# Recurrent-state products on all 128 rows of the matrix engine, and expert results added there: one change to a two-layer hybrid network kernel

## The chip, the cores and the metric

The kernel runs on one core of a Trainium2 chip, as one program of 39,137 instructions. The core has a matrix engine (PE, whose weight loads are listed apart as PEld), three engines for elementwise work (DVE, ACT and POOL), and a sync engine (SP) that here only issues DMAs. The metric is the device time of one execution in microseconds; smaller is better.

## The reference

Two layers over 512 latent and 256 context tokens of width 1024. The parts that the change touches:

```
def gla_scan(q, k, v, la, state):          # 4 heads, keys of 32, values of 64, chunks of 64 tokens
    def step(S, xs):
        b = jnp.cumsum(lc, axis=-2)
        inter = jnp.einsum('bhld,bhde->bhle', qc * jnp.exp(b), S)
        ...
        h = inter + jnp.einsum('bhls,bhse->bhle', att, vc)
        S = jnp.exp(b[..., -1, :])[..., None] * S + jnp.einsum('bhsd,bhse->bhde', kc * jnp.exp(b[..., -1:, :] - b), vc)

def mlstm_scan(q, k, v, ig, lf, state):    # 4 heads of 64
        num = a[..., None] * jnp.einsum('bhld,bhde->bhle', qc, C) + jnp.einsum('bhls,bhse->bhle', s, vc)

def hybrid_layer(...):
    ...
    y = hier_moe(...)                      # every token: the sum of two experts' weighted results
    x_l = post_norm(DN_ALPHA * x_l + g2_l * y_l.reshape(B, S, D), p['ln_ffn_g'], p['ln_ffn_b'])
```

Both scans run over the tokens in both directions (context first, then latents), and the two directions' results are added. Layer 0 gives outputs for all 6 tiles of 128 tokens, layer 1 for the 4 latent tiles only.

## The kernel before

**Order.** The program is written as generators ("threads") that a small planner (`Sched`, `Thread`, `run`) steps by estimated ready times. Beside the gated linear attention (`gla`, called GLA here) and the mLSTM run the input projections (`projections`: long rows of `mm<-whi,hT` matmuls) and the conditioning (`ada`: `mm<-wa,cs`). A compile-time scheduler then fixes the order of each engine's instructions by a simulated timeline. On the chip each engine goes through its own list in order.

**GLA.** `gla_span` does 256 tokens in one direction: four chunks of 64. Head pairs lie on partition halves: rows 0 to 63 hold heads 0 and 1 (g = 0), rows 64 to 127 heads 2 and 3 (g = 1). DVE forms the decays, PE the per-chunk products `pu`, and DVE the chain of states `glS` (lines 1130 to 1139). Then, for each tile of 128 tokens, chunk `cc` and half `g`, two matmuls add into one PSUM region (lines 1179 to 1183): the masked scores `A` (tile `gA`) by the values `v2`, over 128 rows, and the decayed queries `qs` (`Fqs`) by the state that entered the chunk, over the 64 rows of the half:

```
r = slice(64 * g, 64 * g + 64)
nc.tensor.matmul(o, A[:, 2 * g + cc]..., self.v2[:, t, cc, g, :], start=True, stop=ent is None)
nc.tensor.matmul(o, qs[r, 2 * u + cc]..., ent[r, :], start=False, stop=True)
```

**mLSTM.** `mlstm` first runs the states `C` (`mC`) over six tiles in both directions, then goes tile by tile: for each direction and head a 128-row matmul `PT x va` (`mE` by `mva`) and a 64-row one, `qa x C` (`mqa` by `mC`), into one region (lines 1299 to 1302).

All of these operands are float32. Each float32 matmul of the program is two MATMULs, each with a weight load of its own, in the trace.

**End of a layer.** `final_phase` loads, for each tile of 128 tokens, the results of the two experts (`y0`, `y1`; between the layers they lie in spare buffers named `whi`, `wlo`, `wr`), adds them on POOL (line 2151), multiplies by the gate `g2` in layer 0, and does the residual, the norm and (in layer 0) the modulated norm for the next layer. There are 6 tiles after layer 0 and 4 after layer 1. The pool `big` has two PSUM buffers of 128 x 1024.

`tt` and `cp` choose an engine by the planner's clocks (`pick`).

Of the kernel before, what the change touches and what calls it, by code (L numbers as in the profile page):

```python
# [51 lines left out]
def host_consts():  # L52
    import numpy as np
    cols, off, state = [], {}, {"n": 0, "g": None}

    def add(name, a):
        a = np.asarray(a, np.float32)
        if a.ndim == 1:
            a = np.broadcast_to(a, (128, a.shape[0]))
        off[name] = (state["g"], state["n"] - off[state["g"]][0], a.shape[1])  # L60
        cols.append(a)
        state["n"] += a.shape[1]
        off[state["g"]] = (off[state["g"]][0], state["n"] - off[state["g"]][0])

    def group(g):
        state["g"] = g
        off[g] = (state["n"], 0)

    p = np.arange(128)
    group("base")  # L70
    add("ident", np.eye(128))
    add("mk", (p // 32 % 2)[:, None] == np.arange(2)[None, :])
    group("gla")
    add("r64", np.tile((np.arange(64) > 0), 4))
    add("r8", np.tile((np.arange(8) > 0), 32))
    s, l = (p % 64)[:, None, None], np.arange(64)[None, None, :]
    same = (p // 64)[:, None, None] == np.arange(2)[None, :, None]
    for d in range(2):
        a, b = (s, l) if d == 0 else (l, s)
        ms = [(s // 8 == l // 8) & (a <= b)]  # L80
        for w in (8, 16, 32):
            ms.append((s // (2 * w) == l // (2 * w)) & (a // w % 2 == 0) & (b // w % 2 == 1))
        group(f"gm{d}")
        for n, m in enumerate(ms):
            add(f"gm{d}{n}", (m & same).reshape(128, 128))
    group("ml")
    add("negf", np.where(p[:, None] <= p[None, :], 0.0, NEG))
    add("negb", np.where(p[:, None] >= p[None, :], 0.0, NEG))
    for q in range(2):
        sel = np.zeros((128, 128))  # L90
        for m in range(128):
            for d in range(2):
                sel[DB * d + 2 * q + m // 64, m] = 1
        add(f"sel{q}", sel)
    group("da")
    inv = (np.float32(10000.0) ** (-np.arange(16, dtype=np.float32) / np.float32(16))).astype(np.float32)
    t = np.arange(NL)
    ar = (t // 64).astype(np.float32)[:, None] * inv
    ac = (t % 64).astype(np.float32)[:, None] * inv
    ang = np.concatenate([ar, ar, ac, ac], -1).astype(np.float32)  # L100
    sgn = np.concatenate([-np.ones(16), np.ones(16)] * 2).astype(np.float32)
    add("cos", np.cos(ang).reshape(TL, 128, 64).transpose(1, 0, 2).reshape(128, -1))
    add("sin", (np.sin(ang) * sgn).reshape(TL, 128, 64).transpose(1, 0, 2).reshape(128, -1))
    group("tr2")
    add("tri", p[:, None] < p[None, :])
    add("ones", np.ones((128, 128)))
    group("rt")
    add("io32", np.arange(32))
    add("io4", np.arange(4))
    add("tokb", FAR - (np.arange(TT)[None, :] * 128 + p[:, None]))  # L110
    add("iojb", np.arange(256) - FAR)
    add("pcol", p[:, None])
    e = np.arange(32)
    add("kb", np.where(e < 2, 65536.0, 0.0) + 31 - e)
    add("kbc", (np.where(p < 2, 65536.0, 0.0) + 31 - p)[:, None])
    group("moe")
    add("far2", (2.0 * FAR + p // 64)[:, None])
    add("far4", (4.0 * FAR + p // 32)[:, None])
    add("ioj2", np.arange(128) % 64 - FAR)
    add("ioj4", np.arange(128) % 32 - FAR)  # L120
    add("sum4", (p // 64 * 32 + p % 32)[:, None] == np.arange(64)[None, :])
    add("ce", np.tile(e, NB))
    for i in range(2):
        add(f"cb{i}", (np.array(caps(i))[None, :] + 128 * np.arange(NB)[:, None]).reshape(-1))
    arr = np.ascontiguousarray(np.concatenate(cols, 1).astype(np.float32))
    return arr, off
# [120 lines left out]
class Net:  # L247
# [796 lines left out]
    def gla_span(self, d, t0, carry):  # L1044
# [81 lines left out]
        for x in range(n64):  # L1126
            for g in range(2):
                nc.tensor.matmul(pu[64 * g:64 * g + 64, x * 64:x * 64 + 64], kt[:, x, 64 * g:64 * g + 64],
                                 self.v2[:, tiles[x // 2], x % 2, g, :], start=True, stop=True)
        S = self.fw.tile([128, n64, 64], F32, name="glS")  # L1130
        entry = {}
        for x in (range(n64) if d == 0 else range(n64 - 1, -1, -1)):
            entry[x] = carry
            u = pu[:, x * 64:x * 64 + 64]
            if carry is None:
                V.tensor_copy(S[:, x, :], u)
            else:
                V.scalar_tensor_tensor(S[:, x, :], carry, dec[:, x:x + 1], u, op0=OP.mult, op1=OP.add)
            carry = S[:, x, :]
        self.carry = carry  # L1140
        for u, t in enumerate(tiles if live else []):
            yield (kf, qf)
            G = self.big.tile([128, 2, 512], F32, name="big")
# [10 lines left out]
            for n, w in enumerate((64, 8, 16, 32)):  # L1154
# [14 lines left out]
                for hh in range(2):  # L1169
                    r = slice(64 * hh, 64 * hh + 64)  # L1170
                    V.copy_predicated(Aj[r, :, hh], mj[r, None, hh].to_broadcast([64, 4, y, w]), Gj[r])
            yield (A, S)
            po = self.big.tile([128, 2, 512], F32, name="big")
            for cc in range(2):
                ent = entry[2 * u + cc]
                for g in range(2):
                    o = po[:, g, cc * 64:cc * 64 + 64]
                    r = slice(64 * g, 64 * g + 64)
                    nc.tensor.matmul(o, A[:, 2 * g + cc].rearrange("p a l -> p (a l)"), self.v2[:, t, cc, g, :],
                                     start=True, stop=ent is None)  # L1180
                    if ent is not None:
                        nc.tensor.matmul(o, qs[r, 2 * u + cc].rearrange("p a l -> p (a l)"), ent[r, :],
                                         start=False, stop=True)
            src = po[:, :, 0:128].rearrange("p g (c e) -> p c g e", c=2)
            if d == 0:
                self.cp(self.gl[:, t], src, 256)
            else:
                hh = self.fp.tile([128, 256], F32, name="ghh")
                V.tensor_tensor(hh.rearrange("p (c g e) -> p c g e", c=2, g=2), self.gl[:, t], src, op=OP.add)
                f = lambda x: x.rearrange("p c g e -> p (c g e)")  # L1190
                self.head_out(self.fp, hh, 4, 64, f(rs[t]), f(self.gl[:, t]))
                self.dump(f"gl{self.i}_{t}", f(self.gl[:, t]))

    def head_out(self, pw, hh, nh, w, mul, out):

# [13 lines left out]
    def mlstm(self, pg):  # L1209
# [11 lines left out]
            V.tensor_copy(mdec[d], pd[:, :16].rearrange("p (q n) -> p q n", n=8)[:, :, :TT])  # L1221

        orders = [[0, 1, 2, 3, 4, 5], [1, 0, 5, 4, 3, 2]]
        C = pg.tile([128, 2, TT, 2, 65], F32, name="mC")
        prev = [{}, {}]
        pend = []
        for x in range(TT + 1):
# [14 lines left out]
            for d, t, y, kw in pend:  # L1242
                pu = self.tp.tile([128, 512], F32, name="tp")
                for h in range(4):
                    o = (h // 2) * 65
                    nc.tensor.matmul(pu[64 * (h % 2):64 * (h % 2) + 64, o:o + 65], kw[:, h, :], va[:, t, h, :],
                                     start=True, stop=True)
                if y == 0:
                    self.cp(C[:, d, t], pu[:, :130].rearrange("p (q e) -> p q e", q=2), 130)
                else:  # L1250
                    for q in range(2):
                        V.scalar_tensor_tensor(C[:, d, t, q, :], C[:, d, prev[d][t], q, :], mdec[d][:, q, y:y + 1],
                                               pu[:, q * 65:q * 65 + 65], op0=OP.mult, op1=OP.add)
            pend = new

        rev = lambda t: (0 if t == 0 else 0)
        for t in self.otiles:
# [37 lines left out]
            for d in range(2):  # L1295
                first = prev[d][t] is None
                for h in range(4):
                    o = nm[:, h % 2, (2 * d + h // 2) * 65:(2 * d + h // 2) * 65 + 65]
                    nc.tensor.matmul(o, PT[d][:, h % 2, h // 2, :], va[:, t, h, :], start=True, stop=first)
                    if not first:  # L1300
                        r = slice(64 * (h % 2), 64 * (h % 2) + 64)
                        nc.tensor.matmul(o, qa[r, d, h // 2, :], C[r, d, prev[d][t], h // 2, :], start=False, stop=True)
            hs = []
            dn = self.sm.tile([128, 2, 2, 2], F32, name="mdn")
            for d in range(2):
# [803 lines left out]
    def final_phase(self):  # L2109
# [7 lines left out]
        with ExitStack() as st:  # L2117
# [28 lines left out]
            def main():  # L2146
                for n, t in enumerate(tiles):
                    y0, y1, x = nxt[n]
                    if g2:
                        yield (y0, y1, x)  # L2150
                    nc.gpsimd.tensor_tensor(y0, y0, y1, op=OP.add)
                    self.dump(f"moe{i}_{t}", y0)
                    if g2:
                        nc.vector.tensor_tensor(y0, y0, g2[1 if t < TC else 0], op=OP.mult)
                    nc.vector.scalar_tensor_tensor(x, x, ALPHA, y0, op0=OP.mult, op1=OP.add)
                    s6 = self.sm.tile([128, 2, 6], F32, name="s6", bufs=6)
                    for h in range(2):
                        nc.vector.bn_stats(s6[:, h, :], x[:, 512 * h:512 * h + 512])
# [53 lines left out]
```

## Time and profile before

| | us |
|---|---|
| median of 3 runs (lowest to highest) | 2624.3 (2619.9 to 2630.46) |
| the profiled execution, and its span in the trace | 2632.14, 2630.3 |
| PE busy, PEld busy | 2224.2 (85%), 1655.3 (63%) |
| DVE, ACT, POOL busy | 1430.0, 877.0, 669.7 |
| mean granted PE clock | 0.891 |

The granted clock is a share of full speed: 1.00 is 2.4 GHz, 0.50 is 1.2 GHz. A stretch with a value between them had both. A busy PE is not PE at its peak: matmuls overlap and their ends are modelled, so the price of a matmul is read from the distance between starts.

### The profile page before, as it was taken

The numbers are of one execution on the slowest core, as the hardware profiler recorded it, in microseconds if no ns is written. First come the engines' busy times: TensorE is split into PE (matmuls) and PEld (weight loads), VectorE is DVE, ScalarE is ACT, GpSimd is POOL, SyncE is SP. The second block draws the span as 40 slices with busy tenths as digits, with TensorE's granted clock in tenths as the row PEclk, the third lists the DMA queues.
The fourth block names the chain that finished last, engine by engine and source line by source line (L and its number), as shares of the span: only waits on it lengthen the run. The fifth ranks groups of instructions, "written<-read, shape, count | busy, mean of one in ns | idle before, by whom it ended". The sixth has DMA issues, their size and how long they took to land. (4 is left out here: it accounts for less than half of the span.)

```text
span 2630.3 us, 39137 instructions
## 1 busy us (share of the span) xinstructions
PE 2224.2 (85%) x14731; PEld 1655.3 (63%) x14731; DVE 1430.0 (54%) x2876; ACT 877.0 (33%) x1589; POOL 669.7 (25%) x504
## 2 busy tenths in 40 slices
PE   5899999978959999999953789999795999889891
PEld 3687988956846656455522578889674666555440
DVE  4565646367786455454419456544778534344324
ACT  2633212166114344444303624111641423233211
POOL 1222312110123232332314222311103322222313
PEclk9899998979979989999975789979997999989996
DMA  8253452140248889999985553311324887999995
GB/s 245 77 146 98 122 151 70 42 131 22 105 179 310 348 321 392 374 372 380 375 336 165 143 139 97 101 33 37 129 67 194 315 339 310 390 410 407 371 394 233
DMA packets 257752, 583.41 MB, mean 222 GB/s; under 512 B 47220, under 2 KB 187620, under 8 KB 208408
## 3 DMA queue, kind: packets, MB, share of 16 engines
q1 hardware_dynamic: 245368, 559.86, 58.3%
q0 software_dynamic: 12192, 21.01, 2.3%
q8 instruction: 118, 1.93, 0.3%
q14 instruction: 74, 0.61, 0.1%
HBM read 553.02 MB, written 46.27 MB: 228 GB/s over the span
## 5 line engine op out<-in xcount | busy, mean ns | idle before, releaser
L222 PE MATMUL mm<-whi,hT 128*128 128x256 f32 (+2 forms) x2144 | 498.0, 324 | 8.3 <-ACT st L222 4.4
L222 PEld LDWEIGHTS mm<-whi,hT 128*128 128x128 f32 (+1 forms) x2144 | 377.5, 207 | 37.1 <-issue 6.7
L222 DVE TENSOR_TENSOR wlo<-wr,whi 128x1024 fp32r<-128x1024 f32 x217 | 323.8, 1510 | 136.6 <-ACT whi L222 136.1
L222 POOL TENSOR_TENSOR wlo<-wr,whi 128x1024 fp32r<-128x1024 f32 x99 | 248.2, 2511 | 556.9 <-ACT whi L222 331.8
L222 ACT ACTIVATE whi<-wr 128x1024 fp32r<-128x1024 f32 x316 | 321.7, 1054 | 176.5 <-PE mm L222 110.0
L222 PE MATMUL mm<-wlo,hT 128*128 128x256 f32 (+2 forms) x1072 | 345.3, 322 | 6.6 <-POOL wlo L222 4.7
L222 PE MATMUL big<-whi,xT 128*128 128x512 f32 (+1 forms) x800 | 264.7, 407 | 4.4 <-ACT xT L222 4.0
L222 PE MATMUL big<-wr,xT 128*32 128x512 f32 (+1 forms) x1344 | 251.4, 618 | 7.9 <-DMA wr<-in_moe_w_dram 4.9
L222 PEld LDWEIGHTS mm<-wlo,hT 128*128 128x128 f32 (+1 forms) x1072 | 221.4, 207 | 23.8 <-POOL wlo L222 8.3
L222 PEld LDWEIGHTS big<-whi,xT 128*128 128x128 f32 (+1 forms) x800 | 146.8, 187 | 44.7 <-ACT xT L222 5.9
L222 POOL DMA_INDIRECT xg<-fdram,ti x67 | 88.4, 1319 | 329.1 <-DVE ti L222 277.9
L222 PE MATMUL big<-wlo,xT 128*128 128x512 f32 (+1 forms) x400 | 162.6, 406 | 1.2 <-DVE wlo L222 1.2
L222 PEld LDWEIGHTS big<-wr,xT 128*32 128x32 f32 (+1 forms) x1344 | 69.7, 127 | 146.9 <-issue 129.0
L222 PE MATMUL mm<-wr,hT 128*32 128x256 f32 (+1 forms) x1008 | 142.0, 502 | 5.9 <-DMA wr<-in_moe_w_dram 3.0
L222 PE MATMUL tp<-cst_base,xg 32*128 32x32 f32 (+3 forms) x536 | 81.8, 291 | 62.9 <-DVE wt L222 41.5
L222 PEld LDWEIGHTS tp<-cst_base,xg 32*128 32x128 f32 (+3 forms) x536 | 70.6, 199 | 92.8 <-DVE wt L222 47.5
L222 ACT ACTIVATE xT<-tp 128x512 fp32r<-128x512 f32 (+3 forms) x92 | 49.0, 532 | 226.3 <-PE tp L222 202.2
L222 PE MATMUL mm<-hT,whi 128*128 128x512 f32 (+3 forms) x400 | 113.3, 373 | 6.5 <-ACT stg L222 3.4
L222 PE MATMUL mm<-wo,mT 128*128 128x512 f32 x480 | 115.4, 397 | 0.0
L222 DVE SCALAR_TENSOR_TENSOR hT<-hT,tp 128x128 f32<-128x128 f32 (+1 forms) x84 | 29.6, 353 | 152.2 <-ACT hT L222 150.1
L222 POOL DMA_INDIRECT ybuf<-ys,di x67 | 75.0, 1119 | 108.3 <-DVE ys L222 35.0
L222 PEld LDWEIGHTS mm<-wo,mT 128*128 128x128 f32 x480 | 88.9, 188 | 19.6
(374 smaller groups left out, 3795.7 us busy)
## 6 DMA issues: line engine op xcount, KB each, us to landing
wr<-in_moe_w_dram SPq DMA_DIRECT2D x384, 1024.0 KB
wa<-in_w_ada_dram SPq DMA_DIRECT2D x84, 512.0 KB
wr<-in_w_in_dram SPq DMA_DIRECT2D x52, 512.0 KB
hT<-in_w_ada_dram SPq DMA_DIRECT2D x12, 512.0 KB
wor<-in_w_out_dram SPq DMA_DIRECT2D x12, 512.0 KB
xmid<-px SPq DMA_DIRECT2D x10, 512.0 KB
fdram<-mT SPq DMA_DIRECT2D x10, 512.0 KB
x<-xmid SPq DMA_DIRECT2D x10, 512.0 KB
```

Of the source, the lines that this page charges most:

```text
L222: r = f(*a, **kw)
```

## The change

Three parts.

1. **GLA.** After the chain of states, one product per span writes `S2` (`glS2`, 128 x 4 x 2 x 64): the states twice, each copy multiplied by a 0/1 column that clears the rows of the other half. The second matmul then reads all 128 rows of `qs` and of the copy for its half. The states keep one buffer instead of two (`bufs=1`), and POOL copies the last state (`gcr`) and its cleared pair (`gcz`) for the next span.
2. **mLSTM.** The same with `Cz` (still `mC` in the listings), written after each of the first five steps in each direction; the states themselves now alternate between two slots (`mCr`).
3. **Experts' results.** `y0 + y1` becomes four float32 matmuls by the identity into a `big` buffer, from which DVE reads.

```
@@ gla_span @@
-        S = self.fw.tile([128, n64, 64], F32, name="glS")
-        entry = {}
+        S = self.fw.tile([128, n64, 64], F32, name="glS", bufs=1)
+        S2 = self.fw.tile([128, n64, 2, 64], F32, name="glS2", bufs=1)
+        entry, z = {}, self.carry2 if carry is not None else None
         for x in (range(n64) if d == 0 else range(n64 - 1, -1, -1)):
-            entry[x] = carry
+            entry[x] = z
+            z = S2[:, x]
             ...
-        self.carry = carry
+        self.tt(S2, S[:, :, None, :].to_broadcast([128, n64, 2, 64]),
+                self.c("mg")[:, None, :, None].to_broadcast([128, n64, 2, 64]), OP.mult, 512)
         ...
-            yield (A, S)
+            yield (A, S2)
...
-                        nc.tensor.matmul(o, qs[r, 2 * u + cc].rearrange("p a l -> p (a l)"), ent[r, :],
+                        nc.tensor.matmul(o, qs[:, 2 * u + cc].rearrange("p a l -> p (a l)"), ent[:, g, :],
                                          start=False, stop=True)
...
+        self.carry = self.fw.tile([128, 64], F32, name="gcr", bufs=1)
+        nc.gpsimd.tensor_copy(self.carry, carry)
+        self.carry2 = self.fw.tile([128, 2, 64], F32, name="gcz", bufs=1)
+        nc.gpsimd.tensor_copy(self.carry2, z)
@@ mlstm @@
-        C = pg.tile([128, 2, TT, 2, 65], F32, name="mC")
+        Cz = pg.tile([128, 2, TT - 1, 2, 2, 65], F32, name="mC")
+        C = pg.tile([128, 2, 2, 2, 65], F32, name="mCr")
...
+                if y + 1 < TT:
+                    B = [128, 2, 2, 65]
+                    self.tt(Cz[:, d, y], C[:, d, y % 2, :, None, :].to_broadcast(B),
+                            self.c("mh")[:, None, :, None].to_broadcast(B), OP.mult, 260)
...
-                        r = slice(64 * (h % 2), 64 * (h % 2) + 64)
-                        nc.tensor.matmul(o, qa[r, d, h // 2, :], C[r, d, prev[d][t], h // 2, :], start=False, stop=True)
+                        nc.tensor.matmul(o, qa[:, d, h // 2, :], Cz[:, d, orders[d].index(t) - 1, h // 2, h % 2, :], start=False, stop=True)
@@ final_phase @@
+                    yield (y0, y1, x)
+                    sm = self.big.tile([128, 2, 512], F32, name="big")
+                    for h in range(2):
+                        for z, y in enumerate((y0, y1)):
+                            nc.tensor.matmul(sm[:, h, :], self.ident, y[:, 512 * h:512 * h + 512], start=z == 0, stop=z == 1)
+                    sm = sm.rearrange("p a b -> p (a b)")
+                    yield ()
                     if g2:
-                        yield (y0, y1, x)
-                    nc.gpsimd.tensor_tensor(y0, y0, y1, op=OP.add)
-                    self.dump(f"moe{i}_{t}", y0)
-                    if g2:
-                        nc.vector.tensor_tensor(y0, y0, g2[1 if t < TC else 0], op=OP.mult)
-                    nc.vector.scalar_tensor_tensor(x, x, ALPHA, y0, op0=OP.mult, op1=OP.add)
+                        nc.vector.tensor_tensor(y0, sm, g2[1 if t < TC else 0], op=OP.mult)
+                        sm = y0
+                    nc.vector.scalar_tensor_tensor(x, x, ALPHA, sm, op0=OP.mult, op1=OP.add)
```

The scheduler's order moves with it. In the first GLA span of layer 0, PE's list before held the output products of tile 0 (`gA` by the values `v_143`, `Fqs` by the state `glS`) between score matmuls (`Fq,Fk`) and the conditioning:

```order
L222 MATMUL big<-v_143,gA_1169 128x64 x3
L222 MATMUL mm<-wa,cs 32x128 x8
L222 MATMUL big<-Fq,Fk 128x64 x3
L222 MATMUL big<-glS,Fqs 128x64
L222 MATMUL big<-v_143,gA_1169 128x64
L222 MATMUL big<-glS,Fqs 128x64
L222 MATMUL big<-Fq,Fk 128x64 x3
L222 MATMUL tp<-cst_base,adar 128x128
```

Now, with `glS_1404` the cleared copies, the same place reads:

```order
L224 MATMUL big<-v_143,gA_1169 128x64 x3
L224 MATMUL big<-Fq,Fk 128x64 x7
L224 MATMUL mm<-wa,cs 32x128 x2
L224 MATMUL big<-glS_1404,Fqs 128x64
L224 MATMUL big<-v_143,gA_1169 128x64
L224 MATMUL big<-glS_1404,Fqs 128x64
L224 MATMUL mm<-wa,cs 32x128 x6
L224 MATMUL big<-Fq,Fk 128x64 x9
```

These rows now stand one projection group (24 matmuls `mm<-whi,hT`) later in PE's list than before, with ten score matmuls and other work ahead of the first product that needs the copies.

POOL's list in GLA of layer 0, span 3, was this (`Fq` are decayed queries, `wlo` half of a split weight, `stg` and `gA` buffers that are cleared):

```order
L222 TENSOR_TENSOR st<-st,ghalf 128x256
L222 TENSOR_TENSOR wlo<-wr,whi 128x1024
L222 TENSOR_TENSOR Fq<-glq,Fe 128x256
L222 MEMSET stg 128x1 x3
L222 MEMSET gA_1169 128x512
```

and is now this, with the copies `glS_2111` and the two carries:

```order
L224 TENSOR_TENSOR st<-st,ghalf 128x256
L224 TENSOR_TENSOR wlo<-wr,whi 128x1024
L224 TENSOR_TENSOR Fq<-glq,Fe 128x256 x2
L224 TENSOR_TENSOR glS_2111<-glS,cst_gla 128x512
L224 COPY gcr<-glS 128x64
L224 MEMSET stg 128x1 x3
L224 COPY gcz<-glS_2111 128x128
L224 MEMSET gA_1169 128x512
```

The three new instructions stand behind a `wlo` and two `Fq`. Of the 12 spans POOL makes the copies in 10 and DVE in 2; of the 20 `Cz` products POOL makes 9 and DVE 11.

Between the layers, PE's list was this, from the gate rows (`mod`) on:

```order
L222 MATMUL tp<-cst_base,mod_85 128x128 x16
L222 MATMUL tp<-cst_base,prow 128x128
L222 MATMUL mm<-wa,cs 32x128 x24
L222 MATMUL tp<-cst_base,whi 128x128 x8
L222 MATMUL tp<-cst_base,adar 128x128
```

and is now this:

```order
L224 MATMUL tp<-cst_base,mod_85 128x128 x12
L224 MATMUL big<-whi,cst_base 128x512
L224 MATMUL tp<-cst_base,mod_85 128x128 x4
L224 MATMUL big<-whi,cst_base 128x512 x7
L224 MATMUL big<-wlo,cst_base 128x512 x8
L224 MATMUL big<-wr,cst_base 128x512 x4
L224 MATMUL tp<-cst_base,prow 128x128
L224 MATMUL mm<-wa,cs 32x128 x16
L224 MATMUL big<-y_12684,cst_base 128x512
```

The sums of five tiles (four matmuls each) stand ahead of the parameters (`prow`) and of the conditioning.

## Rows read from the trace of the kernel before

**Rows 1.** Windows: busy us (instructions) of PE, PEld, DVE, ACT, POOL; PE clock; DMA share; GB/s.
```profile
140.00:330.00 190.00, 186.58 (x1764) 164.01 (x1762) 124.08 (x276) 59.42 (x139) 52.39 (x52) 0.93 0.44 125
380.00:500.00 120.00, 117.71 (x993) 104.01 (x994) 71.27 (x216) 26.00 (x58) 26.95 (x22) 0.89 0.22 61
1540.00:1700.00 160.00, 151.73 (x1314) 136.59 (x1313) 95.87 (x205) 46.96 (x97) 45.96 (x45) 0.94 0.37 106
1700.00:1810.00 110.00, 104.40 (x738) 93.83 (x738) 59.47 (x166) 20.33 (x39) 22.00 (x18) 0.82 0.13 37
1378.00:1437.00 59.00, 13.00 (x94) 8.12 (x94) 56.38 (x91) 17.15 (x41) 30.46 (x17) 0.50 0.54 177
```
**Rows 2.** Groups of PE by form: rows*columns of the weights, count | busy us, mean ns.
```profile
L222 PE MATMUL big<-mC,mqa 64*128 64x65 f32 x144 | 34.5, 323 | 0.0
L222 PE MATMUL big<-glS,Fqs 64*128 64x64 f32 x152 | 33.7, 303 | 0.0
```
**Rows 3.** Timeline of PE in GLA of layer 0: start us, us, work, count.
```profile
176.32 0.43 PE L222 MATMUL big<-glS,Fqs 64*128 64x64 f32 x2
176.69 0.43 PE L222 MATMUL big<-v,gA 128*128 128x64 f32 x2
177.05 0.43 PE L222 MATMUL big<-glS,Fqs 64*128 64x64 f32 x2
```
**Rows 4.** Timeline of PE in the mLSTM of layer 0.
```profile
411.45 1.00 PE L222 MATMUL big<-mva,mE 128*128 128x65 f32 x8
412.39 0.71 PE L222 MATMUL big<-mqk 64*128 64x128 f32 x8
```
**Rows 5.** Timeline of PE in the mLSTM of layer 1.
```profile
1757.81 0.69 PE L222 MATMUL big<-mva,mE 128*128 128x65 f32 x2
1758.43 0.69 PE L222 MATMUL big<-mC,mqa 64*128 64x65 f32 x2
```
**Rows 6.** Windows of one us around a fall of the clock in that mLSTM.
```profile
1753.00:1754.00 1.00, 1.00 (x7) 0.80 (x7) 0.00 (x0) 0.00 (x0) 0.00 (x0) 0.98 0.00 0
1754.00:1755.00 1.00, 1.00 (x5) 0.88 (x5) 0.91 (x4) 0.00 (x0) 0.00 (x0) 0.50 0.00 0
```
**Rows 7.** Groups of POOL by form: count | busy us, mean ns | idle before.
```profile
L222 POOL TENSOR_TENSOR Fks<-glk,Fe 128x512 f32<-128x512 f32 x10 | 14.3, 1433 | 32.1 <-PE tp L222 22.7 <-ACT Fe L222 9.4
L222 POOL TENSOR_TENSOR mh<-mh,mh 128x256 f32<-128x256 f32 x10 | 7.3, 730 | 94.4 <-DVE mh L222 94.4
L222 POOL COPY gp<-g 32x256 f32<-32x256 f32 x4 | 1.7, 416 | 0.1
```
**Rows 8.** Timeline of DVE: the end of a chain of states; a 256-column product.
```profile
172.17 0.27 DVE L222 SCALAR_TENSOR_TENSOR glS<-glS,gdec,tp 128x64 f32<-128x64 f32 x1
...
1699.81 0.42 DVE L222 TENSOR_TENSOR hsq<-ghh 128x256 f32<-128x256 f32 x1
```
**Rows 9.** Timeline of POOL and DVE between the layers.
```profile
1377.51 2.33 POOL L222 TENSOR_TENSOR whi<-whi 128x1024 f32<-128x1024 f32 x1 [4.61 <-DMA whi<-ybuf]
1381.14 3.24 DVE L222 SCALAR_TENSOR_TENSOR x<-x,whi 128x1024 f32<-128x1024 f32 x1
1392.25 6.63 DVE L222 TENSOR_TENSOR wlo<-wlo,g 128x1024 f32<-128x1024 f32 x2
1401.27 1.21 DVE L222 SCALAR_TENSOR_TENSOR x<-x,wlo 128x1024 f32<-128x1024 f32 x1
```
**Rows 10.** Timeline of PE: float32 matmuls of 512 columns on four column groups.
```profile
1330.28 1.92 PE L222 MATMUL big<-wr,xT 128*32 128x512 f32 x16
```
**Rows 11.** Windows of one us: PE starts a dense row at half clock.
```profile
1437.00:1438.00 1.00, 0.57 (x3) 0.57 (x4) 1.00 (x4) 0.00 (x0) 0.96 (x2) 0.50 0.10 32
1443.00:1444.00 1.00, 1.00 (x27) 0.50 (x17) 0.96 (x5) 0.51 (x2) 0.00 (x0) 0.83 0.38 152
```
**Rows 12.** Timeline of DVE at the end: one operation beside a POOL add, and without.
```profile
2610.08 2.82 DVE L222 TENSOR_TENSOR x<-x,ln_ffn_b 128x512 f32<-128x512 f32 x1
2612.89 0.68 DVE L222 TENSOR_TENSOR x<-x,ln_ffn_b 128x512 f32<-128x512 f32 x1
```

More of the change, by code (lines that the diff above doesn't have):

```diff
@@ L75, in host_consts @@
     add("r8", np.tile((np.arange(8) > 0), 32))
+    add("mg", (p // 64)[:, None] == np.arange(2)[None, :])
     s, l = (p % 64)[:, None, None], np.arange(64)[None, None, :]
@@ L86, in host_consts @@
     group("ml")
+    add("mh", (p // 64)[:, None] == np.arange(2)[None, :])
     add("negf", np.where(p[:, None] <= p[None, :], 0.0, NEG))
@@ L1177, in gla_span @@
                     o = po[:, g, cc * 64:cc * 64 + 64]
-                    r = slice(64 * g, 64 * g + 64)
                     nc.tensor.matmul(o, A[:, 2 * g + cc].rearrange("p a l -> p (a l)"), self.v2[:, t, cc, g, :],
@@ L1248, in mlstm @@
                 if y == 0:
-                    self.cp(C[:, d, t], pu[:, :130].rearrange("p (q e) -> p q e", q=2), 130)
+                    self.cp(C[:, d, 0], pu[:, :130].rearrange("p (q e) -> p q e", q=2), 130)
                 else:
                     for q in range(2):
-                        V.scalar_tensor_tensor(C[:, d, t, q, :], C[:, d, prev[d][t], q, :], mdec[d][:, q, y:y + 1],
+                        V.scalar_tensor_tensor(C[:, d, y % 2, q, :], C[:, d, 1 - y % 2, q, :], mdec[d][:, q, y:y + 1],
                                                pu[:, q * 65:q * 65 + 65], op0=OP.mult, op1=OP.add)
+                if y + 1 < TT:
+                    B = [128, 2, 2, 65]
+                    self.tt(Cz[:, d, y], C[:, d, y % 2, :, None, :].to_broadcast(B),
+                            self.c("mh")[:, None, :, None].to_broadcast(B), OP.mult, 260)
             pend = new
```

## The prediction

> **What bounds the kernel now.** I read the windows first, because the change touches three places and the time of each has its own limit. In GLA and mLSTM of both layers (four stretches, 580 us together) PE is busy for 186.58 of 190, 117.71 of 120, 151.73 of 160 and 104.40 of 110 us, with DVE at 54 to 65% of each stretch, POOL at 20 to 29% and the DMA engines at 13 to 44% [rows 1]. So PE sets the pace there: 560 of 580 us, and what makes its list shorter makes the stretch shorter, as long as nothing else comes late. Second, the granted clock in the same windows is 0.93, 0.89, 0.94 and 0.82 [rows 1]: PE is full of work and still spends a part of the time at 1.2 instead of 2.4 GHz. Third, the stretch between the layers is another matter: PE has 13.00 us of work in 59, at half clock throughout, and DVE is busy for 56.38 [rows 1]. That stretch is DVE's, and so is the end of the program.
>
> Then the timeline, for the price of one matmul. A float32 matmul is two instructions in it. Where a 128-row product alternates with a 64-row one, each pair of instructions takes 0.36 to 0.37 us from start to start, whichever it is: 176.32, 176.69, 177.05 [rows 3]. Where 128-row products of nearly the same shape (65 columns for 64) follow each other, eight instructions go from 411.45 to 412.39, 0.94 us, or 0.118 each instead of 0.182 [rows 4]. That run includes the step to the 64-row product behind it. So it is the change between 128 and 64 rows that costs, not the size.
>
> **The products with the states.** There are 152 and 144 such 64-row instructions [rows 2], so 148 products of the program (76 in GLA, 72 in mLSTM), each behind a 128-row partner. One such couple takes 4 x 0.182 = 0.73 us now. With every operand on 128 rows it should take 4 x 0.118 = 0.47. The difference, 0.26 us, times 148 is 38 us at full clock. Both ends: 0 if the couple keeps its price; for the other, the couples at half clock, which take 0.62 us per two instructions or 1.24 each [rows 5], and lose 0.77 if they also come to full speed. Counting such rows in the timeline, some 14 of them are so, which adds 14 x 0.5 = 7, so 45. PE idles for 3% of the four stretches, and a shorter list will meet a few producers that were just in time; I take nine tenths: **-34 us**.
>
> **The clock.** The mean clocks above mean 190 x 0.07 + 120 x 0.11 + 160 x 0.06 + 110 x 0.18 = 56 us of full-speed work lost, 33 of them in the two mLSTM stretches. In layer 1 the clock fell from 0.98 to 0.50 within one us while PE was busy without a gap, in a row of just these alternating couples [rows 6], and the couples went on at half speed [rows 5]. In such a row the array stands still during more than a third of the time, since each weight load waits. Packed rows of 128-row products leave less of that. No row shows how the clock takes the new sequence. The ends are -33 (the mLSTM keeps full clock) and +10 (shorter work, more waiting for others, as much clock lost again as a third of that); the transposes and the 4- and 64-row score products that remain in the same rows speak for little. I take **-10 us**.
>
> **What the copies cost.** POOL makes 10 of the 12 `S2` products and 12 pairs of carries, 9 `Cz` products; DVE the rest. A 128x512 product takes POOL 1.43 us, a 128x256 one 0.73, a small copy 0.42 [rows 7]; that is 10 x 1.43 + 12 x (0.42 + 0.73, the bound for the larger copy) + 9 x 0.73 = 35 us of POOL, in stretches where it is idle for more than two thirds. On DVE, 11 products of 0.42 [rows 8] and two of about twice that are 6.3 us. Neither engine bounds. On the path they count where a product needs the copy at once. In GLA the last state was ready at 172.17 + 0.27 = 172.44 [rows 8] and PE reached the first product with it at 176.32 [rows 3]: 3.9 us of cover for a copy of 1.43. The first span had nearly no cover, and its order moves the products behind a projection group. The new carry `gcr` makes DVE wait for POOL at the head of the next span's chain, with everything queued behind it on DVE; the next chain begins only after this span's scores, masks and products, so it is done by then. In mLSTM the two slots make each state update wait for the copy of two steps before, 0.73 on POOL. I take **+4 us**: DVE's eleven products stand in the serial chain of states at the head of mLSTM, where PE has other work only in part. The ends are 0 and the +66 of the slow rival below.
>
> **The experts' sums.** On PE one instruction of 512 columns takes at most 0.48 us at full clock, since 16 on four column groups, four in a row on each, took 1.92 [rows 10]; 0.96 at half. A tile has eight: 3.8 or 7.7 us, against 2.33 for the first add on POOL [rows 9]. PE enters at half clock. Elsewhere a dense row that began at 1437 at 0.50 saw the clock rise during 1443 to 1444 [rows 11], so six us pass: 6.3 instructions, and the rest at 0.48, 6.8 us in all. DVE starts 4.5 us later. What it gets back: beside POOL's adds its own operations were stretched, two residual steps to 3.24 (one row of the two shown) and two gate products to 6.63, where 1.21 each is the undisturbed time [rows 9], so 2 x 2.0 + 4.2 = 8.2 us. The third and fourth sums wait for a `big` buffer that DVE has to read first; I charge 2. Between the layers: -8.2 + 4.5 + 2, **-2 us**, with ends at -8 (PE hidden) and +8 (PE's clock stays low). At the end of the program three DVE operations were stretched in the same way, by 4 us in all (one of them 2.82 beside 0.68 [rows 12]); the first sum costs the same 4.5 more. **0 us** there, ends -3 and +11: four tiles at half clock need 31 us of PE before the last tile's work on DVE starts. What hides the sums in the first place is DVE's 9.4 us per tile (56.38 over six tiles); a sum of 7.7 is just below it.
>
> **Sum.** The profiled execution took 2632.1 us, 1.8 more than its span. 2632.1 - 34 - 10 + 4 - 2 = 2590. That execution lies 7.8 above the median of the runs, 2624.3, so I forecast 2582.
>
> **The rivals.**
>
> *The couples keep their price.* If a weight load may only run under a matmul on other rows, 128-row products always conflict, and the new couples take 0.73 like the old ones. Then the first two terms go, and the time is 2624.3 + 4 - 2, about 2626. Against it stand the eight 128-row instructions at 0.118, which share all rows [rows 4]; 0.182 each would have been 1.46 us. The Trainium skill states this rule ("TensorE: Matmul & The Clock Gate", "Part 3: Packing small matmuls": weight loads overlap with matmuls in flight only when the row group differs). By that rule the products gain 0 us; by the row, 38. The trace does not agree with it here. Chance 0.06.
>
> *Half of it is lost to others.* With PE's list shorter, the products of a tile wait for the masks and decays on DVE and ACT. DVE at 65% in GLA [rows 1] leaves room, but its work comes in bursts. With half of the 44 us gone the time is 2604. Chance 0.13.
>
> *The clock stays up.* If mLSTM keeps 2.4 GHz, the clock term is -33 instead of -10: 2559. For it: the fall sits in rows of the couples themselves [rows 6]. Against: what else stands there is not denser than before. Chance 0.15.
>
> *PE waits for the copies (slower).* POOL goes through its list in order, and the copy stands behind weight splits and query products. If in each of the 12 spans it begins 8 us after the chain ends, PE stands for 8 + 1.43 - 3.9 = 5.5 us per span, 66 in all: 2582 + 66 = 2648. The point from which it decides is a delay at which these waits eat the 42 us of gain, 3.5 per span, so a POOL that starts the copy 6 us late every time. Against: POOL is busy for 52.39 of 190 us there [rows 1], and the order keeps filler between. Chance 0.04.
>
> **How the numbers follow.** The forecast's own case has 0.62 and spans 2565 to 2597. The range of 2552 to 2611 takes in most of the cases with half the gain or a full clock, and leaves out the two without a gain. Less than 0.5%, 13 us, cannot be told from no change here: faster means below 2611. The forecast, the clock case and nearly all of the half case are faster, 0.86 with some of it kept back for what no row shows; same 0.09, from the first rival and the edge of the half case; slower 0.05.
>
> **What would show it.** In the new trace the couples should start every 0.24 us per two instructions, and GLA and mLSTM should each end earlier by about 0.26 us per couple. The clock of the mLSTM windows should be above 0.89 and 0.82. POOL's adds should be gone and DVE's residual steps between the layers back at 1.2 us, with the first of them some 4 us later. The forecast is wrong if the couples stay at 0.36, if PE shows waits on POOL before products with `glS2` or `mC`, or if PE's sums between the layers run at half clock and DVE waits for each.

## The result, and the profile after

The changed kernel takes 2562.9 us (median of 4 runs, 2560.8 to 2568.6), the kernel before beside it 2624.7. The ratio is 0.9767, 95% interval 0.9742 to 0.9793: 61 us less. The profiled execution took 2560.8 us, its span 2559.0, at a mean clock of 0.914 (0.891 before).

The page after, busy time first, then the row of the granted clock in 40 slices:

```profile
PE 2192.1 (86%) x14811; PEld 1623.5 (63%) x14811; DVE 1428.6 (56%) x2889; ACT 876.0 (34%) x1589; POOL 661.2 (26%) x537
...
PEclk9899999989969999999986789999996989889997
```

The two traces lie further apart than the medians, 71 us by their spans (2630.3 and 2559.0), because the profiled execution of the kernel before was 7.5 us above its median. PE's busy sum fell by 32 us only, less than half of these 71. The rest must be looked for in stretches. I cut both traces at the same pieces of work. Windows of the kernel before, columns as in [rows 1]: GLA of layer 0, the mLSTM's chain of states, its outputs, the stretch between the layers, and then GLA, chain and outputs of layer 1:

```profile
137.00:334.40 197.40, 193.11 (x1810) 169.42 (x1809) 127.05 (x285) 61.02 (x143) 53.80 (x54) 0.93 0.44 125
334.40:392.60 58.20, 54.07 (x532) 48.26 (x531) 26.03 (x74) 6.65 (x12) 9.46 (x10) 0.94 0.51 146
392.60:497.20 104.60, 103.90 (x812) 92.73 (x813) 64.25 (x191) 24.15 (x55) 26.60 (x22) 0.87 0.17 48
1372.40:1434.80 62.40, 15.12 (x92) 10.23 (x92) 55.56 (x87) 17.72 (x40) 29.46 (x16) 0.50 0.59 197
1531.40:1699.30 167.90, 159.63 (x1421) 143.47 (x1421) 100.58 (x220) 49.51 (x105) 47.32 (x46) 0.95 0.38 106
1699.30:1745.40 46.10, 41.33 (x365) 37.92 (x364) 23.09 (x61) 6.75 (x10) 10.94 (x7) 0.89 0.30 86
1745.40:1813.20 67.80, 66.97 (x406) 59.81 (x405) 40.19 (x110) 14.29 (x30) 13.02 (x12) 0.77 0.01 3
```

The same seven of the changed kernel:

```profile
132.20:324.00 191.80, 181.05 (x1812) 160.97 (x1811) 127.08 (x285) 60.95 (x143) 64.75 (x71) 0.96 0.45 129
324.10:387.80 63.70, 59.34 (x573) 54.11 (x573) 27.20 (x81) 7.31 (x14) 13.85 (x16) 0.94 0.47 135
387.80:466.40 78.60, 77.21 (x770) 72.03 (x771) 62.17 (x188) 22.95 (x52) 26.65 (x22) 1.00 0.22 64
1342.20:1398.90 56.70, 37.28 (x141) 19.58 (x141) 46.41 (x87) 17.50 (x40) 11.28 (x10) 0.71 0.66 217
1495.30:1651.70 156.40, 150.08 (x1413) 138.06 (x1413) 103.77 (x221) 49.38 (x104) 54.18 (x60) 0.97 0.40 113
1651.70:1699.60 47.90, 43.09 (x392) 39.19 (x391) 27.64 (x69) 7.35 (x11) 13.50 (x13) 0.93 0.30 86
1699.60:1745.20 45.60, 43.14 (x381) 40.98 (x380) 39.73 (x103) 13.70 (x29) 12.96 (x12) 1.00 0.01 4
```

The outputs of the mLSTM are the large pieces: 26 and 22 us shorter, with the clock at 1.00 instead of 0.87 and 0.77. The counts warn against reading one row alone: 42 instructions went from the outputs of layer 0 (812 to 770) and 41 came into the chain ahead of them (532 to 573). Chain and outputs together went from 162.8 to 142.3 and from 113.9 to 93.5: 20.5 and 20.4 us. GLA gave 5.6 and 11.5, the stretch between the layers 5.7, the end of the program 1.7. That is 65 of the 71; the rest lies in stretches that no edit touches.

The couples in the changed trace (timeline of PE in the mLSTM of layer 0, answering to [rows 3]):

```profile
393.47 0.39 PE L224 MATMUL big<-mC,mqa 128*128 128x65 f32 x2
393.69 0.39 PE L224 MATMUL big<-mva,mE 128*128 128x65 f32 x2
393.92 0.39 PE L224 MATMUL big<-mC,mqa 128*128 128x65 f32 x2
```

PE's two groups that answer to [rows 2]:

```profile
L224 PE MATMUL big<-mC,mqa 128*128 128x65 f32 x144 | 27.7, 274 | 0.0
...
L224 PE MATMUL big<-glS,Fqs 128*128 128x64 f32 x120 | 24.8, 291 | 0.0
```

(76 GLA products are 152 instructions; the other 32 read the carry `gcz`.) Two instructions now start every 0.222 us instead of 0.364; a couple takes 0.444 instead of 0.73. The mean of one instruction fell only from 323 to 274 ns [rows 2]: as matmuls overlap, the starts tell the price and the means do not.

The traces also show where an old couple lost its time. First two matmuls at a change of depth in the kernel before, taken from inside [rows 3], then the weight loads of the same two:

```profile
176.48 0.27 PE L222 MATMUL big<-glS,Fqs 64*128 64x64 f32 x1
176.69 0.32 PE L222 MATMUL big<-v,gA 128*128 128x64 f32 x1
```

```profile
176.43 0.19 PEld L222 LDWEIGHTS big<-glS,Fqs 64*128 64x128 f32 x1
176.68 0.19 PEld L222 LDWEIGHTS big<-v,gA 128*128 128x128 f32 x1
```

And two weight loads of the changed kernel, where the depth stays the same:

```profile
393.52 0.19 PEld L224 LDWEIGHTS big<-mC,mqa 128*128 128x128 f32 x1
393.63 0.19 PEld L224 LDWEIGHTS big<-mva,mE 128*128 128x128 f32 x1
```

With one depth a load starts 0.11 us after the load before it. At the change it starts 0.25 after, together with its matmul, and 0.20 after the matmul before. From 176.32, 176.48 and 176.69 the two steps of a pair are 0.16 and 0.20 us, where 0.111 each is the step within one depth: 0.14 us more per change of depth.

### The profile page after: what moved, and what is told of

It reads as the page before. It is cut to its first block, busy times and chain, and to the rows that moved or that the text cites. A ratio compares the mean times of both kernels' runs of the same rounds, so it can differ in the third digit from the quotient of the medians.

```text
span 2559.0 us, 39336 instructions
## 1 busy us (share of the span) xinstructions
PE 2192.1 (86%) x14811; PEld 1623.5 (63%) x14811; DVE 1428.6 (56%) x2889; ACT 876.0 (34%) x1589; POOL 661.2 (26%) x537
## 5 line engine op out<-in xcount | busy, mean ns | idle before, releaser
L224 PE MATMUL mm<-whi,hT 128*128 128x256 f32 (+2 forms) x2144 | 482.9, 317 | 11.2 <-ACT st L224 3.8
L224 PEld LDWEIGHTS mm<-whi,hT 128*128 128x128 f32 (+1 forms) x2144 | 363.4, 199 | 40.4 <-issue 6.3
L224 PE MATMUL mm<-wlo,hT 128*128 128x256 f32 (+2 forms) x1072 | 336.3, 314 | 6.6 <-POOL wlo L224 4.5
L224 PEld LDWEIGHTS mm<-wlo,hT 128*128 128x128 f32 (+1 forms) x1072 | 212.7, 198 | 23.2 <-POOL wlo L224 8.1
```

Of the source, the lines that this page charges most:

```text
L224: r = f(*a, **kw)
```

## The experiments

Gains are worked out from the ratio to the runs of the kernel before beside each experiment (medians 2620.7 to 2626.0).

| kernel | median, us | ratio to before, 95% interval | gain, us |
|---|---|---|---|
| before, mLSTM part alone | 2578.9 | 0.9827 (0.9805 to 0.985) | 45 |
| before, GLA part alone | 2605.6 | 0.9938 (0.9918 to 0.9958) | 16 |
| before, sums alone | 2612.7 | 0.9966 (0.9949 to 0.9983) | 9 |
| before, regrouped | 2558.2 | 0.9753 (0.9734 to 0.9771) | 65 |
| before, regrouped, with sums | 2550.2 | 0.9718 (0.9691 to 0.9745) | 74 |
| changed, 72 extra products on 64 rows | 2638.6 | 1.0059 (1.0037 to 1.0081) | -15 |
| changed, 72 extra products on 128 rows | 2581.2 | 0.9834 (0.9807 to 0.986) | 44 |
| changed, copies twice | 2571.0 | 0.9791 (0.9762 to 0.9819) | 55 |
| before, results added on DVE | 2616.2 | 0.9971 (0.995 to 0.9992) | 8 |
| changed, grouped | 2552.5 | 0.9735 (0.9701 to 0.977) | 69 |
| changed, grouped, again | 2559.0 | 0.9749 (0.9729 to 0.9768) | 66 |
| changed, again | 2559.1 | 0.9758 (0.9737 to 0.9779) | 64 |

One caution on single traces: the experts of layer 1, which no edit touches, took 731 to 748 us over these profiled executions. Whole times are therefore compared by medians, and traces stretch by stretch.

**The three parts, each alone on the kernel before.** Edits: the diff's hunks in `mlstm`, in `gla_span`, or in `final_phase`.

```
 mLSTM part:  + Cz ...    nc.tensor.matmul(o, qa[:, d, h // 2, :], Cz[:, d, ...], ...)
 GLA part:    + S2, gcr, gcz ...    nc.tensor.matmul(o, qs[:, 2 * u + cc]..., ent[:, g, :], ...)
 sums part:   - nc.gpsimd.tensor_tensor(y0, y0, y1, op=OP.add)
              + nc.tensor.matmul(sm[:, h, :], self.ident, y[...], start=z == 0, stop=z == 1)
```

> The kernel before with only the mLSTM part (cleared copies Cz, 128-row products). From the two traces, the mLSTM output stretches went from 104.6 to 78.6 us and from 67.8 to 45.6 us: 48 us in all, of which 72 couples at 0.26 explain 19. Theory A (the alternation of row depths cost both the 0.26 per couple and the clock): this part alone brings about 48 us, 2577 us, and the clock stays at 1.00 through both mLSTM stretches. Rival B (the couples only cost their 0.26; the clock came back because of what else had changed in the program, the earlier GLA or another order): about 19 us, 2606, clock near 0.87 and 0.77 as before. Rival C (the copies cost on their own): less than 19.

> The kernel before with only the GLA part (S2, gcr, gcz, 128-row products). In the two traces the GLA stretches shrank by 5.6 and 11.5 us, 17 together, where 76 couples at 0.26 make 20. Theory A: about 17 us, 2607; the couples start every 0.22 to 0.24 us per two instructions. Rival B (POOL's copies or the carries make PE wait): 2615 to 2630, with PE waiting on POOL ahead of the state products. Rival C (most of the whole gain hangs on GLA, because it sets in which state of the clock the mLSTM begins): 40 us or more, 2585, with a higher clock in the mLSTM stretches.

> The kernel before with only the experts' sums on the matrix engine. Theory A, from the two traces: 2.4 us between the layers and 1.7 at the end, 4 us in all, 2620, within 0.5% of before. Rival B (the sums carry a good part, because POOL no longer stretches DVE's operations; 8 us between the layers and 4 at the end): 2612. Rival C (PE at half clock holds DVE up, tile by tile): 2630 to 2635.

Gains of 45, 16 and 9 add up to 70, against 61 for all three (64 beside other runs of the kernel before); the intervals, some 5 us either way on each, are wide enough for that. The mLSTM part is the bulk. Its 72 couples at 0.286 make 21 us, so the rest, some 24, came by another way than the couple's price; the windows above point to the clock. In its profiled execution (13.6 us above its median) layer 0 went to 1.00, but layer 1 only from 0.77 to 0.84, short of the 1.00 that theory A asked for: rival B is refuted for layer 0. Two traces of another kernel, the changed one in the grouped order (below), show what happened in layer 1; there, too, all these products have 128 rows. From the first product of layer 1's outputs to the last, in the first and in the second of its traces:

```profile
1702.30:1739.00 36.70, 36.10 (x326) 34.81 (x326) 30.98 (x84) 11.08 (x23) 10.63 (x10) 1.00 0.01 2
```

```profile
1707.80:1750.50 42.70, 42.70 (x326) 41.51 (x325) 30.81 (x84) 11.06 (x23) 10.50 (x10) 0.82 0.01 1
```

In the second the clock had fallen at 1706.2, ahead of these products. PE had just had gaps (the first window here); so it had in the mLSTM part's trace, where the clock fell at 1733.9 (the second):

```profile
1702.00:1706.00 4.00, 2.25 (x26) 1.61 (x26) 3.05 (x12) 0.75 (x2) 1.84 (x2) 1.00 0.00 0
```

```profile
1730.00:1734.00 4.00, 2.26 (x26) 1.48 (x24) 3.01 (x11) 0.61 (x2) 1.85 (x2) 0.99 0.00 0
```

So one and the same kernel can enter layer 1's outputs at either level, and its two traces differ by 6 us in that stretch. The first had such gaps too (2.60 us busy of the four from 1698) and kept 1.00; why the clock fell in the one and not in the other stays open.

The GLA part came out as theory A said: the mLSTM's clocks stayed near 0.86 and 0.77 in its trace. The sums gave 9 (4 to 13 by the interval) rather than 4: rival B's 2612. Theory A's 4 counted 2.4 us between the layers, where the windows above have 5.7; 5.7 + 1.7 = 7.4 fits. In its own trace that stretch is 55.3 us long (62.4 before).

**Regrouped: 64 rows kept, no copies.** In each tile all products with the values come first, then all with the states; one `start` per PSUM bank, since the products of a bank now stay open together.

```
-   matmul(o, PT[d][...], va[...], start=True, stop=first)
-   if not first: matmul(o, qa[r, d, ...], C[r, d, ...], start=False, stop=True)
+ for d, h: matmul(o, PT[d][...], va[...], start=d == 0 and h < 2, ...)
+ for d, h: if not first: matmul(o, qa[r, d, ...], C[r, d, ...], start=False, ...)      (GLA alike)
```

> The kernel before, without copies and without sums on PE: the state products keep their 64 rows, but stand behind all 128-row products of their tile (4 and 4 in GLA, 8 and 8 in mLSTM), on alternating halves of the rows. Theory A (what cost was the change between 128 and 64 rows at every step, and the clock fell for that reason): the change of depth comes once per tile instead of once per product, so 0.26 or more is saved per couple (the 64-row score products on alternating halves go faster than 0.11 per instruction), and the clock stays up: at least the 65 us of the two state parts, 2560 or below. Rival B (the couples get shorter, but 64-row rows use half of the array and the clock falls as before): 38 to 52 us less work in PE, no clock: 2572 to 2590, with mLSTM clocks near 0.87 and 0.77. Rival C (a 64-row product costs 0.18 per instruction whatever stands beside it): within 0.5% of before.

2558.2 us: the whole gain of the change, with none of its three parts. PE's timeline in it, in the mLSTM of layer 0:

```profile
406.56 1.00 PE L222 MATMUL big<-mva,mE 128*128 128x65 f32 x8
407.49 1.11 PE L222 MATMUL big<-mC,mqa 64*128 64x65 f32 x16
408.43 0.67 PE L222 MATMUL big<-mqk 64*128 64x128 f32 x8
```

The windows of its two output stretches:

```profile
381.20:462.00 80.80, 77.81 (x811) 72.58 (x812) 63.74 (x191) 24.02 (x54) 27.50 (x22) 1.00 0.22 62
...
1700.50:1749.90 49.40, 47.13 (x403) 44.86 (x404) 40.06 (x110) 13.97 (x30) 14.13 (x12) 0.90 0.01 3
```

Eight 128-row instructions take 0.93 us, 16 64-row ones 0.94: 0.116 and 0.059 each. The 64-row ones are cheaper because they go by twos. At the step from the one group to the other (timeline cut at 407.50):

```profile
407.28 0.28 PE L222 MATMUL big<-mva,mE 128*128 128x65 f32 x1
407.49 0.33 PE L222 MATMUL big<-mC,mqa 64*128 64x65 f32 x2
```

Two of them start within 0.01 us of each other, and the pairs follow every 0.11 to 0.12 us: the time of one 128-row instruction serves both halves of the rows. (The change of depth in these two lines takes 0.21 us, as in the kernel before.) A couple is now 2 x 0.116 + 2 x 0.059 = 0.35, 0.38 less than before. Of that, 2 x 0.14 = 0.28 are the two changes of depth, and 0.10 is the sharing of the halves, which a lone 64-row product in a couple can't have. Rivals B and C fall: with 64-row products too the clock stays up, wholly in layer 0 and for the most part in layer 1. The edit changes the `start` flags as well; they are the same in the grouped kernel below, which gains nothing clear by them.

**The alternation brought back, and a control.** On the changed kernel, 72 redundant products.

```
+ nc.tensor.matmul(nm[:, h % 2, 300:365], qa[r, d, h // 2, :], Cz[r, d, ...], start=True, stop=True)
  (control: qa[:, d, ...], Cz[:, d, ...], all rows)
```

> The changed kernel with 72 redundant products in mLSTM: behind each 128-row state product one more on the 64 rows of its half, into unused columns of the same buffer (no result changes). The order of row depths is then 128, 128, 64, 128, 128, 64. Theory A (each change of row depth leaves the array standing while a weight load waits, and the clock falls in rows that are full of that): the couple grows by about 0.5 us (two changes at 0.19 and two instructions at 0.06), 36 us, and the clock of the mLSTM stretches falls from 1.00 toward 0.87 and 0.77, up to 29 us more: 2600 to 2628. Rival B (the clock was lost for another reason, so that it stays at 1.00): 36 us at most, 2585 to 2599.

> The control: the same 72 redundant products, but on all 128 rows, so that there is no change of row depth. Theory A: 72 times 0.22 makes 16 us, the clock in mLSTM stays at 1.00: 2579. Rival B (any longer row of such products costs the clock): clock below 0.95 in the mLSTM stretches and 2590 or more.

The two differ in the row depth of 72 products, and by 57 us. The control is 18 us above the changed kernel, close to the 72 x 0.22 = 16 of its work. With 64 rows, the windows of the output stretches:

```profile
395.90:517.20 121.30, 120.78 (x873) 107.94 (x874) 62.93 (x188) 23.13 (x53) 27.90 (x22) 0.79 0.15 42
...
1748.60:1831.40 82.80, 81.64 (x443) 73.11 (x442) 39.21 (x107) 13.81 (x29) 14.16 (x13) 0.67 0.01 2
```

A piece of PE's timeline in the first of them:

```profile
403.21 0.44 PE L224 MATMUL big<-mva,mE 128*128 128x65 f32 x2
403.48 0.75 PE L224 MATMUL big<-mC,mqa 128*128 128x65 f32 x4
404.16 0.43 PE L224 MATMUL big<-mva,mE 128*128 128x65 f32 x2
```

And the windows of the control's two stretches:

```profile
390.30:481.70 91.40, 89.28 (x872) 83.56 (x873) 61.88 (x188) 23.34 (x53) 27.00 (x22) 1.00 0.20 57
...
1710.90:1762.90 52.00, 49.87 (x441) 47.93 (x442) 39.49 (x106) 13.94 (x29) 13.58 (x13) 1.00 0.01 2
```

The step from one couple to the next is 404.16 - 403.21 = 0.95 us, as 0.14 per change gives (6 instructions at 0.111 and two changes make 0.67 + 0.28 = 0.95). By the same count a product on 64 rows that stands alone adds 0.22 + 0.28 = 0.50 us, 36 us for the 72. And the clock falls below what it was in the kernel before, 0.79 and 0.67, where the control keeps 1.00 with the same number of instructions. Where it falls in layer 0, PE is busy without a gap, in a row of alternating couples; windows of one us there:

```profile
404.00:405.00 1.00, 1.00 (x10) 0.86 (x11) 0.00 (x0) 0.00 (x0) 0.00 (x0) 1.00 0.30 72
405.00:406.00 1.00, 1.00 (x10) 0.88 (x8) 0.44 (x3) 0.24 (x2) 0.00 (x0) 0.52 0.08 16
```

The other traces agree. Five have couples that alternate (the kernel before, the GLA part, the sums part, the results on DVE, the extra products on 64 rows). Between the first and the last product of layer 0's outputs the clock fell 23 times in them, each time with PE busy without a gap right before. In the nine traces without alternation, the regrouped kernels' included, it fell there once, behind gaps (copies twice). In layer 1 gaps come into it: in the kernel before PE was busy for 0.48 and 0.68 us in the two us from 1749, and the fall of [rows 6] came at 1754, 2.6 us into the couples. But the clock then stayed down for 27 us in the four traces with the old couples and for 34 with the extra products, where in those traces without alternation in which it fell there it was back after 7 to 17.

So the alternation costs twice: 0.14 us per change, and the clock. Theory A's top of 2628 was still 11 too low: the kernel is 76 us above the changed one, of which 36 are the products' own, and the 40 that are left for the clock are more than the 29 I allowed.

**Grouped at one depth.** The changed kernel with the regrouped order, still on 128 rows.

```
  regrouped order as above, with qs[:, ...], ent[:, g, :] and qa[:, ...], Cz[:, ...]
```

> The changed kernel, copies and 128-row products included, with the products of a tile in the grouped order (all products with the values first, then all with the states). Theory A (only a change of row depth costs, and the order among products of one depth is nothing): as the changed kernel, 0.976 to 0.978 of before, 2560 to 2566. The 12 us by which the regrouped kernel with sums is faster are then the copies (about 7 us by the stretch from the GLA's last output to the mLSTM's first) and the shorter 64-row instructions (0.06 against 0.11). Rival B (the grouped order itself is worth something): 2550.

> The changed kernel again, beside its grouped twin on the same chip and the same runs of the kernel before. Theory A (grouping products of one depth is worth nothing; the 10 us between the two came from runs on different occasions): 0.974 to 0.976 of before for both, within 4 us of each other. Rival B (the grouped order is worth something in itself): the changed kernel at 0.977, some 2562, and its twin 8 to 10 us below it.

> The grouped twin of the changed kernel again (128-row products, all with the values first, then all with the states). Theory A: within 4 us of the changed kernel beside it. Rival B: 8 to 10 us below it, 0.973 of before, some 2552.

The first runs gave 2552.5, as rival B had it. Side by side on one occasion the two take 2559.1 and 2559.0, as theory A had it. By the ratios the grouped order is 2 us better there (0.9749 for 0.9758) and 8 better in the first runs (0.9735 for 0.9767), and all four intervals overlap: no gain from the order among products of one depth is shown, and one of a few us isn't excluded.

**Copies twice.** Each copy of the changed kernel is written a second time.

```
  self.tt(S2, ...)        + nc.gpsimd.tensor_tensor(S2, ...)
  self.tt(Cz[:, d, y], ...)   + nc.vector.tensor_tensor(Cz[:, d, y], ...)
```

> The changed kernel with every cleared copy written twice: the second S2 on POOL (1.14 us, 12 of them), the second Cz on DVE (0.5 us, 20 of them). Theory A (the copies are hidden): within 5 us of the changed kernel, 2558 to 2568. Rival B (they stand on the path): 12 times 1.14 and 20 times 0.5 make 24 us, 2585. In between, with the difference in one of the two stretches: that stretch's copies are the ones on the path, and so is their price in the change itself.

The median is 8 to 12 us above the changed kernel's two, the ratio 6 to 9 us above with touching intervals: in between, and not sharp. In the one trace both chains of the mLSTM grew (63.7 to 68.3, 47.9 to 53.5), while GLA of layer 1 did not (156.4 to 152.5):

```profile
330.70:399.00 68.30, 62.95 (x600) 56.57 (x600) 32.58 (x92) 8.30 (x16) 16.96 (x17) 0.92 0.44 130
1664.10:1717.60 53.50, 46.96 (x396) 42.46 (x396) 32.95 (x79) 7.95 (x12) 15.93 (x14) 0.90 0.27 77
```

But PE has 27 more instructions in the first of these, so a part is work moved by the scheduler, and the clock differs too: 0.92 and 0.90 here for 0.94 and 0.93, and 1.00 in that GLA for 0.97. That the `Cz` copies bear a price of a few us, and `S2` none, is likely from this and not shown.

**Results added on DVE.** The kernel before, with `nc.vector` for `nc.gpsimd` in the add.

> The kernel before, with the experts' results added on DVE in place of POOL (ten more operations of 1.2 us on DVE, none on POOL; PE untouched). Theory A (the sums on PE gain because POOL's adds stretched DVE's own operations, 9 us between the layers and 4 at the end): the stretching goes, and the 12 us that DVE now has to add itself use it up: within 0.5% of before, 2610 to 2632. Rival B (DVE was not held up by POOL; the sums on PE gain for another reason): DVE, which is the bound there, pays its 12 us in full: 2634 or more.

A gain of 8 us, the same as that of the sums on PE within the intervals, although DVE does ten operations more. The stretch between the layers is 57.8 us (62.4 before). DVE's groups in it, two of the adds, two gate products and two residual steps:

```profile
L222 DVE TENSOR_TENSOR wlo<-wlo 128x1024 f32<-128x1024 f32 x2 | 2.4, 1212 | 0.0
L222 DVE TENSOR_TENSOR wlo<-wlo,g 128x1024 f32<-128x1024 f32 x2 | 2.4, 1209 | 0.0
...
L222 DVE SCALAR_TENSOR_TENSOR x<-x,whi 128x1024 f32<-128x1024 f32 x2 | 2.4, 1195 | 0.0
```

The two gate products take 2.4 us where they took 6.63 beside POOL's adds, the two residual steps 2.4 for two of 3.24 [rows 9]. So the stretching beside POOL's adds is what the sums' gain comes from; between PE and DVE as the engine that takes the adds over, these runs show no difference.

**Regrouped, with the sums.** The best of both.

> The regrouped kernel (64-row products behind all 128-row ones of their tile, no copies) together with the experts' sums on the matrix engine. If the two gains add up, as they sit in different stretches: 62 + 8 = 70 us off 2621, 2551 us, which would beat both kernels. Rival: once the sums enter at another place in the clock's history, their gain between the layers is gone: 2558, like the regrouped kernel alone. Second rival: the sums disturb the order: 2565 or more.

2550.2 us, within 1 us of what was expected: the two gains add up. It has the lowest median of all kernels run. Against the changed kernel (0.9758 and 0.9767) its interval still touches theirs at the edge, so 9 to 13 us better is likely and not proved.

## Why the prediction was right in direction and 19 us off

**The couples (-34): right.** The trace gives 0.444 per couple for the forecast 0.47, and 148 x 0.286 = 42. GLA of layer 0 lost a part of its share, as the nine tenths allowed: 44 couples make 12.6 us, and it became 5.6 shorter. PE's idle time there grew from 4.3 to 10.8 us, with 4.8 us of waits for DVE's masks (`gA`) that the kernel before did not have:

```profile
PE big L224 <- DVE gA L224: 4.8, 3, 3.7
```

The reason was right as well (the change of depth costs, not the size), and the experiments sharpened it: the load at a change starts late, 0.14 us per change, and 64-row products are not slow, they go by twos when grouped. The first rival fell with the first timeline, where 128-row products on the same rows follow each other every 0.111 us.

**The clock (-10): mis-sized, the largest miss.** "Packed rows of 128-row products leave less of that. No row shows how the clock takes the new sequence ... I take -10 us." The rows of its fall stood in the alternation itself, [rows 6] and [rows 5]; I held against it that what else stands there is no denser than before. That was no reason: the extra 64-row products show that the alternation takes the clock away, and the control that as many products of one depth don't. Chain and outputs together became 41 us shorter; the couples make 72 x 0.286 = 21 of them, and 20 are left (for the mLSTM part alone 45 - 21 = 24). The clock can carry them: mean clocks of 0.87 and 0.77 are 27 and 31 us at half speed, where a couple took 1.24 instead of 0.73 [rows 5], and at that ratio full speed saves 58 x (1 - 0.73 / 1.24) = 24. GLA's clock rose too, 0.93 to 0.96 and 0.95 to 0.97. The rival in which the clock stays up, at 2559, is what came, in kind. That its number fits to 4 us is in part luck: its clock term of 33 took all work to go twice as fast at full speed, which the couples do not (0.73 for 1.24), and was some 9 too large, while the sums in it were 7 too small.

**The copies (+4): not settled.** PE shows no wait for POOL ahead of the products with the states, so the slow rival fell. Twice the copies cost 6 to 12 us, partly by moved work; what the copies cost once, no run shows.

**The sums (-2 and 0): mis-sized.** Alone they gave 9. The forecast had DVE's recovery right (8.2 us; the groups of the changed trace below), but charged 4.5 for PE at half clock and 2 for buffers:

```profile
L224 DVE TENSOR_TENSOR wlo<-big,g 128x1024 f32<-128x1024 f32 x2 | 2.4, 1208 | 0.0
...
L224 DVE SCALAR_TENSOR_TENSOR x<-x,whi 128x1024 f32<-128x1024 f32 x2 | 2.5, 1225 | 0.0
```

PE at the first sum, in its timeline:

```profile
1345.46 1.27 PE L224 MATMUL big<-whi,cst_base 128*128 128x512 f32 x2 [0.24 <-DMA whi<-ybuf]
```

DVE's first operation on it:

```profile
1349.84 1.23 DVE L224 TENSOR_TENSOR whi<-big,g 128x1024 f32<-128x1024 f32 x1 [3.89 <-PE big L224]
```

DVE began 4.4 us after the sum, where before it began 2.4 after the add (1377.51 to 1379.88): 2 us later, not 4.5. The clock was at 1.00 one us after the sums began; the gate's transposes stood right ahead of them, and PE had been busy since 1342.2 but for 0.24 us (windows of one us):

```profile
1344.00:1345.00 1.00, 1.00 (x5) 0.71 (x4) 0.05 (x1) 0.60 (x1) 0.00 (x0) 0.50 1.06 422
...
1346.00:1347.00 1.00, 1.00 (x6) 0.57 (x5) 0.00 (x0) 0.00 (x0) 0.00 (x0) 1.00 1.05 430
```

With -24 for the clock in place of -10 and -9 for the sums in place of -2, the same sum gives 2582 - 14 - 7 = 2561.

## What to carry to other kernels

Look in PE's timeline for products of different row depth that alternate: the starts tell what a change of depth costs, and the granted clock over such a row whether it costs the clock as well. Before copies are made to equalise the depth, try the order: all products of one depth first, then those of the other, accumulating in the same bank. And before an operation is moved from POOL to the matrix engine, see whether DVE beside it is stretched; here DVE itself did as well as PE.

## What was not expected of the hardware

Two 64-row float32 instructions on the two halves of the rows start within 0.01 us and together take the time of one 128-row instruction (0.059 us each for 0.116). A change of depth costs 0.14 us more than a step within one depth; the weight load there starts only 0.20 us after the matmul before. The clock fell from 1.00 to 0.52 within an us in rows where PE showed no gap, when 72 64-row products stood among 128-row ones, and stayed at 1.00 when the same products had 128 rows. The regrouped kernel's layer 1 (0.90) lost some clock in another way: from 1712 to 1714 us PE was busy for 0.56 of 2, with a wait of 1.4 us for DVE, and in the next two us the clock fell to 0.97 and then 0.50.
